# Storing the last image of a dilated convolution: sixteen rows of it cut after partition 119, four rows after partition 123

## The chip, the core and the metric

The kernel runs on one core of a Trainium2 chip. The core has a matrix engine (TensorE, PE in the profile, with its weight loads as PEld), a vector engine (VectorE, DVE), a scalar engine (ScalarE, ACT), a general engine (GpSimd, POOL), a queue engine (SyncE, SP) and 16 DMA engines that move data between the chip's main memory (HBM) and the on-chip memory (SBUF, 128 partitions). Matrix products land in PSUM, also 128 partitions, and are copied from there to SBUF by VectorE or ScalarE.

The metric is the device time of one execution in microseconds, the median of three runs. The profile is one further execution, recorded by the hardware profiler.

## What is computed

A 3 x 3 convolution with dilation 2 and zero padding of 2: 16 images of 64 channels and 64 x 64 pixels, 128 output channels, all in float32 at the ends.

```python
output = np.zeros((batch, c_out, h, w), dtype=np.float32)
for b in range(batch):
    for co in range(c_out):
        for ci in range(c_in):
            for kh in range(k):
                for kw in range(k):
                    output[b, co] += weight[co, ci, kh, kw] * x_pad[b, ci, kh*dilation:kh*dilation+h, kw*dilation:kw*dilation+w]
```

The result is 16 x 128 x 64 x 64 floats, 33.55 MB; the input x is 16.78 MB and the weight 0.29 MB.

## The kernel before

**Tiling.** Images are taken in pairs: the 64 channels of the even image lie on partitions 0 to 63, those of the odd image on 64 to 127, so one pair is a tile of 128 partitions x 4096 floats (`x32`). Eight pairs (`pb` 0 to 7) times four groups of 16 rows (`g` 0 to 3) give 32 rounds `G`. The output tile `o_tiles[pb]` has the 128 output channels on its partitions and both images of the pair one behind the other (`m` 0 and 1), 4096 floats each. So a store of R rows of one image moves, on each partition, R x 64 floats, or R x 256 bytes in one piece.

**A round.** With dilation 2 the rows go in blocks of two, and an output block needs the input blocks before it, at it and behind it. The kernel computes two output blocks (`e` 0 and 1) with five products of the weights in place of six: `psP` is the middle weight row times the sum of an even and an odd block (`rowsum`, line 86, on VectorE); `psA` and `psB` hold the rest for the two (`product`, line 172). ScalarE casts x to float16 (line 74) and copies `psP` to SBUF (line 234); VectorE adds it to `psA` and `psB` and writes the output tile (line 241).

**DMAs.** All of them are issued on SP's queue in the order of the program, which is written by hand (a manual schedule): loads of x (`load`, line 65), stores (`store`, line 186, one per image and range of rows, and `store_both`, line 192, two images in one). `store` takes a list `rows` of partition ranges and issues one DMA for each of them. Each issue waits on SP until what it stores has been written. It also waits until the semaphore that it will count on is free: eight of them are used in turn, so a DMA waits for the one issued eight before it to have landed.

**The last pair.** Pairs 3 to 6 store each image whole when the pair is done (2 MB each). The last pair (`pb` 7, images 14 and 15) stores in halves: at `g` 1 rows 0 to 32 of each image, at `g` 3 rows 32 to 64. Rows 0 to 32 of image 15 go in three DMAs: rows 0 to 24 over all 128 partitions, then rows 24 to 32 (`ROWS4` is 8) over partitions 0 to 123 and over 124 to 127 (`FOUR`, line 197). Rows 32 to 64 of both images then follow over 128 partitions, and nothing comes after them.

Of the kernel before, what the change touches and what calls it, by code (L numbers as in the profile page):

```python
# [10 lines left out]
def kernel(  # L11
# [17 lines left out]
    P = 128  # L29
# [6 lines left out]
    GR = 16  # L36
# [24 lines left out]
    def load(pb, cuts=(0, H)):  # L61
        if pb not in x32_tiles:
            x32_tiles[pb] = fpool.tile([P, HW], f32, tag="x32", name="x32")
        for lo, hi in zip(cuts[:-1], cuts[1:]):
            nc.sync.dma_start(  # L65
                out=x32_tiles[pb][:, lo * W : hi * W], in_=x_pair[pb, :, lo * W : hi * W]
            )
# [10 lines left out]
    def rowsum(c):  # L78
        pb, g = divmod(c, NG)
        if g == 0:  # L80
            xs_tiles[pb] = sxpool.tile([P, HW // 2], f16, tag="xs", name="xs")
        v = x16_tiles[pb][:, g * GR * W : (g + 1) * GR * W].rearrange(
            "p (b e q) -> p b e q", e=2, q=2 * W
        )
        s = xs_tiles[pb][:, g * NH : (g + 1) * NH].rearrange("p (b q) -> p b q", q=2 * W)
        nc.vector.tensor_tensor(out=s, in0=v[:, :, 0], in1=v[:, :, 1], op=add)  # L86
# [67 lines left out]
    def casts(G):  # L154
        for n in range(2 if G else 3):
            c = ahead[0]
            if c >= ngroups or c > G + (7 if c < 2 * NG else 5):
                return
            cast(c)
            ahead[0] += 1  # L160

    def product(ps, src, kind, blk0, nblk, first, last):
        for j in (1, 0, 2):
            dw = (j - 1) * d
            o0, o1 = max(0, -dw), W - max(0, dw)
            t = kind * KW + j
            for hb in range(2):
                pp = slice(hb * CI, (hb + 1) * CI)
                rhs = src(pp, dw + o0, dw + o1)
                po = ps[:, hb * NH + blk0 * 2 * W : hb * NH + (blk0 + nblk) * 2 * W]  # L170
                po = po.rearrange("p (r w) -> p r w", w=W)[:, :, o0:o1]
                nc.tensor.matmul(  # L172
                    out=po,
                    lhsT=w_sb[pp, t * CO : (t + 1) * CO],
                    rhs=rhs,
                    start=first and j == 1,
                    stop=last and j == 2,
                )

    def blocks(x16, b0, n, e):  # L180
        v = x16.rearrange("p (b e r w) -> p b e r w", e=2, r=2, w=W)
        return lambda pp, c0, c1: v[pp, b0 : b0 + n, e, :, c0:c1]

    def store(pb, m, r0=0, r1=H, rows=((0, P),)):
        for lo, hi in rows:
            nc.sync.dma_start(
                out=out_img[2 * pb + m, lo:hi, r0 * W : r1 * W],
                in_=o_tiles[pb][lo:hi, m * HW + r0 * W : m * HW + r1 * W],
            )

    def store_both(pb, r0, r1):
        nc.sync.dma_start(
            out=out_img[2 * pb : 2 * pb + 2, :, r0 * W : r1 * W].rearrange("m o q -> o m q"),
            in_=o_tiles[pb].rearrange("p (m q) -> p m q", m=2)[:, :, r0 * W : r1 * W],
        )

    FOUR = ((0, P - 4), (P - 4, P))
    ROWS4 = 8

    for G in range(ngroups):  # L200
        pb, g = divmod(G, NG)
        x16 = x16_tiles[pb]
        xs = xs_tiles[pb].rearrange("p (r w) -> p r w", w=W)
        if g == 0:
            o_tiles[pb] = opool.tile([P, 2 * HW], f32, tag="osb", name="osb")
        o = o_tiles[pb].rearrange("p (m b e q) -> p m b e q", m=2, e=2, q=2 * W)
        b0 = g * NBLK

        def summed():
            ps = ppool.tile([P, 2 * NH], f32, tag="p", name="psP")  # L210
            sv = lambda pp, c0, c1: xs[pp, g * GR // 2 : (g + 1) * GR // 2, c0:c1]
            product(ps, sv, 0, 0, NBLK, True, True)
            return ps

        if G:
            psP = summed()

        psA = apool.tile([P, 2 * NH], f32, tag="ab", name="psA")
        product(psA, blocks(x16, b0, NBLK, 1), 1, 0, NBLK, True, False)
        z = 1 if g == 0 else 0  # L220
        product(psA, blocks(x16, b0 + z - 1, NBLK - z, 1), 2, z, NBLK - z, False, True)

        psB = apool.tile([P, 2 * NH], f32, tag="ab", name="psB")
        product(psB, blocks(x16, b0, NBLK, 0), 3, 0, NBLK, True, False)
        z = 1 if g == NG - 1 else 0
        product(psB, blocks(x16, b0 + 1, NBLK - z, 0), 4, 0, NBLK - z, False, True)

        if not G:
            psP = summed()

        if not G:
            casts(0)
        p_sb = spool.tile([P, 2 * NH], f32, tag="psb", name="p_sb")
        nc.scalar.copy(out=p_sb, in_=psP)  # L234
        if G:
            casts(G)
        if G + 1 < ngroups:
            rowsum(G + 1)
        pv = p_sb.rearrange("p (m b q) -> p m b q", m=2, q=2 * W)
        for e, ps in ((0, psA), (1, psB)):  # L240
            nc.vector.tensor_tensor(  # L241
                out=o[:, :, b0 : b0 + NBLK, e],
                in0=ps.rearrange("p (m b q) -> p m b q", m=2, q=2 * W),
                in1=pv,
                op=add,
            )

        if G == 0:
            load(XF, (0, H // 2))
        if pb == 0:  # L250
            if g % 2 == 1:
                store_both(0, (g - 1) * GR, (g + 1) * GR)
                if g == 1:
                    load(XF, (H // 2, H))
                else:
                    load(XF + 1)
        elif g == NG - 1 and pb == 1:
            store(1, 0)
            store(1, 1, 0, H // 2)
            load(XF + 2)  # L260
            store(1, 1, H // 2, H)
        elif g == NG - 1 and pb == 2:
            store(2, 0)
            load(XF + 3)
            store(2, 1)
            load(XF + 4)
        elif pb == npairs - 1:
            if g % 2 == 1:
                store(pb, 0, (g - 1) * GR, (g + 1) * GR)
                if g == 1:  # L270
                    store(pb, 1, 0, 2 * GR - ROWS4)
                    store(pb, 1, 2 * GR - ROWS4, 2 * GR, FOUR)
                else:
                    store(pb, 1, (g - 1) * GR, (g + 1) * GR)
        elif g == NG - 1:
            store(pb, 0)
            store(pb, 1)
# [37 lines left out]
```

## Time and profile before

| What | Value |
|---|---|
| median of three runs | 126.85 us (126.62, 126.85, 127.08) |
| the profiled execution's span, first to last instruction | 125.0 us |
| PE busy | 105.8 us (85% of the span) |
| DVE busy | 91.0 us (73%) |
| ACT busy | 64.9 us (52%) |
| HBM read, written | 17.07 MB, 33.55 MB: 405 GB/s over the span |
| DMA packets, mean rate | 4722, 406 GB/s |
| stores of 2 MB, issue to landing | 14.9 us (13 of them) |

The span is measured from the first to the last instruction; the median of the runs is the whole execution as the device counts it, so it is longer. "Issue to landing" is the median time from the DMA's issue on SP to its last piece being counted. A packet is one contiguous piece that one of the 16 DMA engines moves; a DMA also leaves a packet of 4 bytes that counts up its semaphore. The busy share of the 16 engines is written in tenths in each of 40 slices of the span.

### The profile page before, as it was taken

The page shows a single profiled execution, that of the slowest core. Times are in us where ns is not written, and L with a number is a line of the kernel's source. Part 1 is how long each engine was busy: PE and PEld are TensorE (multiplying, and loading weights), DVE is VectorE, ACT ScalarE, POOL GpSimd, SP SyncE. Part 2 cuts the span into 40 slices and gives each one's busy share as a digit, 9 for nine tenths or more (in the row PEclk, how much of TensorE's full clock was granted, in tenths as well). Part 3 has the DMA queues.
Part 4 walks back from the last instruction along what each step waited for, and adds up shares of the span by engine and source line. Part 5 has one row for each costly group of instructions (what it writes and reads, how often), then busy time and mean ns, then how long its engine had stood idle before and what let it go on. Part 6 is the DMA issues. An engine that isn't in the chain of part 4 may idle for free.

```text
span 125.0 us, 2343 instructions
## 1 busy us (share of the span) xinstructions
PE 105.8 (85%) x1002; PEld 57.0 (46%) x1002; DVE 91.0 (73%) x103; ACT 64.9 (52%) x68; POOL 2.2 (2%) x8
## 2 busy tenths in 40 slices
PE   6996999999999999999999999999999999600000
PEld 2353555555555555555555555555555555200000
DVE  0561998988898889888988898889888988700000
ACT  4188896665666566656665666566653333100000
POOL 2400000000000000000000000000000000000000
PEclk9999999999999999999999999999999999985555
DMA  5999999999999999999999999999999999999991
GB/s 142 368 450 435 430 401 315 430 422 420 443 427 435 412 441 438 401 435 435 425 430 427 420 435 430 435 420 435 420 430 430 430 425 435 430 414 412 420 395 73
DMA packets 4722, 50.78 MB, mean 406 GB/s; under 512 B 488, under 2 KB 488, under 8 KB 1000
## 3 DMA queue, kind: packets, MB, share of 16 engines
q1 hardware_dynamic: 4712, 50.63, 96.7%
q8 instruction: 8, 0.13, 0.4%
q14 instruction: 2, 0.02, 0.0%
HBM read 17.07 MB, written 33.55 MB: 405 GB/s over the span
## 4 chain that ended last, share of the span: by engine, by line
PE 76%; DMA 6%; ACT 2%; DVE 1%; DVEq 1%; SPq 1%; issue 0%
PE psA L172 31%; PE psB L172 30%; PE psP L172 16%; DMA x<-in_x_dram 6%; ACT x L74 2%; DVE osb L241 1%; DVEq L310 1%; ACT p_sb L234 1%; SPq L65 0%; SPq L89 0%; DVEq L241 0%
## 5 line engine op out<-in xcount | busy, mean ns | idle before, releaser
L172 PEld LDWEIGHTS <-w_sb 64*128 64x128 f16 x960 | 54.6, 94 | 45.8 <-issue 1.4
L234 ACT COPY p_sb<-psP 128x1024 f32<-128x1024 f32 x32 | 32.4, 1012 | 36.9 <-issue 21.5
L241 DVE TENSOR_TENSOR osb<-psA,p_sb 128x1024 f32<-128x1024 f32 x32 | 39.2, 1225 | 13.4 <-PE psA L172 9.8
L172 PE MATMUL psA<-x,w_sb 64*128 64x496 f16 (+3 forms) x384 | 45.1, 365 | 0.0
L172 PE MATMUL psB<-x,w_sb 64*128 64x496 f16 (+3 forms) x384 | 45.1, 365 | 0.0
L241 DVE TENSOR_TENSOR osb<-psB,p_sb 128x1024 f32<-128x1024 f32 x32 | 39.1, 1222 | 0.0
L74 ACT CAST x<-x 128x1024 f16<-128x1024 f32 (+2 forms) x31 | 32.1, 1044 | 0.5 <-DMA x<-in_x_dram 0.3
L172 PE MATMUL psP<-xs,w_sb 64*128 64x496 f16 (+1 forms) x192 | 26.0, 371 | 1.1 <-ACT p_sb L234 1.1
L86 DVE TENSOR_TENSOR xs<-x 128x512 f16<-128x512 f16 x32 | 13.3, 416 | 0.4 <-ACT x L74 0.4
L102 PE MATMUL dm<-zero 128*128 128x512 f16 x12 | 5.3, 579 | 1.2 <-DVE zero L94 1.2
L102 PEld LDWEIGHTS <-zero 128*128 128x128 f16 x12 | 1.4, 128 | 3.2 <-issue 1.8
L112 DVE CAST wd<-w 128x192 f16<-128x192 f32 x1 | 0.5, 503 | 2.4 <-DMA w<-in_weight_dram 2.4
L125 PEld LDWEIGHTS <-wd 128*64 128x64 f16 x30 | 1.0, 118 | 1.8 <-DVE wd L112 0.8
L137 ACT CAST w_sb<-wt 128x384 f16<-128x384 f32 x1 | 0.5, 478 | 2.3 <-PE wt L125 2.3
L114 ACT ACT_TABLE_LOAD x1 | 1.3, 1283 | 0.7 <-PEq L296 0.7
L125 PE MATMUL wt<-ident,wd 128*64 128x128 f16 x30 | 1.6, 241 | 0.0
L114 ACT CAST wd<-w 128x192 f16<-128x192 f32 x1 | 0.5, 539 | 1.5 <-DMA w<-in_weight_dram 1.5
L139 DVE CAST w_sb<-wt 128x384 f16<-128x384 f32 x1 | 0.6, 557 | 0.7 <-PE wt L125 0.7
L135 DVE CAST w_sb<-wt 128x384 f16<-128x384 f32 x1 | 0.6, 558 | 0.5 <-PE wt L125 0.5
L94 DVE MEMSET zero<- 128x256 uint32 x1 | 0.3, 272 | 0.9 <-PEq L296 0.9
L113 POOL TENSOR_TENSOR wd<-w 128x192 f16<-128x192 f32 x1 | 0.8, 799 | 2.3 <-DMA w<-in_weight_dram 2.3
L116 POOL CAST wd<-w 128x192 f16<-128x192 f32 x1 | 0.8, 806 | 0.0
(11 smaller groups left out, 3.8 us busy)
## 6 DMA issues: line engine op xcount, KB each, us to landing
out_dram<-osb SPq DMA_DIRECT2D x13, 2048.0 KB, 14.9
x<-in_x_dram SPq DMA_DIRECT2D x6, 2048.0 KB, 17.0
out_dram<-osb SPq DMA_DIRECT2D x5, 1024.0 KB, 13.1
x<-in_x_dram SPq DMA_DIRECT2D x2, 1024.0 KB, 13.2
x<-in_x_dram SPq DMA_DIRECT2D x1, 1088.0 KB, 5.6
x<-in_x_dram SPq DMA_DIRECT2D x1, 960.0 KB, 7.4
out_dram<-osb SPq DMA_DIRECT2D x1, 768.0 KB, 15.4
w<-in_weight_dram SPq DMA_DIRECT2D x1, 288.0 KB, 2.8
```

Of the source, the lines that this page charges most:

```text
L74: nc.scalar.copy(out=x16_tiles[pb][:, lo * W : hi * W], in_=x32_tiles[pb][:, lo * W : hi * W])
L86: nc.vector.tensor_tensor(out=s, in0=v[:, :, 0], in1=v[:, :, 1], op=add)
L102: nc.tensor.matmul(out=dm[:, 0:512], lhsT=zero[:, 0:P], rhs=zero)
L113: nc.gpsimd.tensor_tensor(out=wdv[:, 3], in0=wv[:, 0], in1=wv[:, 1], op=sub)
L114: nc.scalar.copy(out=wdv[:, 2], in_=wv[:, 0])
L116: nc.gpsimd.tensor_copy(out=wdv[:, 4], in_=wv[:, 2])
L125: nc.tensor.matmul(out=wts[k % 3][r * CI : (r + 1) * CI, c0 + j * CO : c0 + (j + 1) * CO], lhsT=wd[:, t * CI : (t + 1) * CI], rhs=ident,)
L135: nc.vector.tensor_copy(out=t0[0], in_=t0[1])
L172: nc.tensor.matmul(out=po, lhsT=w_sb[pp, t * CO : (t + 1) * CO], rhs=rhs, start=first and j == 1, stop=last and j == 2,)
L234: nc.scalar.copy(out=p_sb, in_=psP)
L241: nc.vector.tensor_tensor(out=o[:, :, b0 : b0 + NBLK, e], in0=ps.rearrange("p (m b q) -> p m b q", m=2, q=2 * W), in1=pv, op=add,)
L310: with _tile.TileContext(nc) as tc:
```

## The change

Rows 0 to 32 of image 15 go in five DMAs instead of three: rows 0 to 12 over 128 partitions (3 KB on each), rows 12 to 28 over partitions 0 to 119 and over 120 to 127 (4 KB on each), rows 28 to 32 over partitions 0 to 123 and over 124 to 127 (1 KB on each). The same bytes are stored. Nothing else differs on any engine; the lines behind line 197 move down by one, and those behind the stores by three.

```diff
     FOUR = ((0, P - 4), (P - 4, P))
-    ROWS4 = 8
+    FIFTEEN = ((0, P - 8), (P - 8, P))
+    ROWS4, ROWS15 = 4, 16
...
                 store(pb, 0, (g - 1) * GR, (g + 1) * GR)
                 if g == 1:
-                    store(pb, 1, 0, 2 * GR - ROWS4)
-                    store(pb, 1, 2 * GR - ROWS4, 2 * GR, FOUR)
+                    cuts = (0, 2 * GR - ROWS15 - ROWS4, 2 * GR - ROWS4, 2 * GR)
+                    store(pb, 1, cuts[0], cuts[1])
+                    store(pb, 1, cuts[1], cuts[2], FIFTEEN)
+                    store(pb, 1, cuts[2], cuts[3], FOUR)
                 else:
                     store(pb, 1, (g - 1) * GR, (g + 1) * GR)
```

## The prediction

> **What bounds the kernel now.** I read the page's head and its slices first, then its chain, then the end of the timeline, then the waits of SP, then the DMA rows. The page:
>
> ```profile
> span 125.0 us, 2343 instructions
> ...
> DMA  5999999999999999999999999999999999999991
> ...
> DMA packets 4722, 50.78 MB, mean 406 GB/s; under 512 B 488, under 2 KB 488, under 8 KB 1000
> ...
> q1 hardware_dynamic: 4712, 50.63, 96.7%
> ...
> PE 76%; DMA 6%; ACT 2%; DVE 1%; DVEq 1%; SPq 1%; issue 0%
> ...
> out_dram<-osb SPq DMA_DIRECT2D x1, 248.0 KB
> out_dram<-osb SPq DMA_DIRECT2D x1, 8.0 KB
> ```
>
> The chain gives PE 76%, but it starts from the last computing instruction, and that is not the end. The timeline's end, with the SP waits from 95 us on:
>
> ```profile
> 108.25 1.22 DVE L241 TENSOR_TENSOR osb<-psB,p_sb 128x1024 f32<-128x1024 f32 x1
> 109.49 1.08 SPq L186 DMA_DIRECT2D out_dram<-osb  x2
> ...
> SPq L310 <- DMA out_dram<-osb: 13.2, 3, 8.5
> ```
>
> Work on the engines ends at 109.47 us, the last stores are issued by 110.57, and then SP waits 13.2 us for stores to land. The 16 DMA engines are busy from 3 us on and are about 12 to 15 us behind all through the end. So the end is the moment when the *last of the 16* has emptied its queue. Windows one 8 KB packet (0.31 us) wide show them stop one after another:
>
> ```profile
> 120.05:120.36 0.31, 0.00 (x0) 0.00 (x0) 0.00 (x0) 0.00 (x0) 0.00 (x0) 0.50 0.94 396
> ...
> 120.98:121.29 0.31, 0.00 (x0) 0.00 (x0) 0.00 (x0) 0.00 (x0) 0.00 (x0) 0.50 0.82 344
> ...
> 121.91:122.22 0.31, 0.00 (x0) 0.00 (x0) 0.00 (x0) 0.00 (x0) 0.00 (x0) 0.50 0.44 185
> ...
> 122.84:123.15 0.31, 0.00 (x0) 0.00 (x0) 0.00 (x0) 0.00 (x0) 0.00 (x0) 0.50 0.25 106
> ...
> 123.46:123.77 0.31, 0.00 (x0) 0.00 (x0) 0.00 (x0) 0.00 (x0) 0.00 (x0) 0.50 0.07 26
> ```
>
> The last two columns are the share of 16 engines and GB/s. GB/s x 0.31 us / 8192 B is the packets begun, so the engines still at work: 15, 13, 7, 4, 1. Three us pass between the first engine out and the last.
>
> **Which engine is late.** The 124-row and the 4-row store use four engines each: every store leaves one packet of 4 B for each engine that it uses, and 488 such packets are 30 DMAs x 16 + 2 x 4. 124 and 4 rows are 31 and 1 on each of four. In the trace's packet records each packet starts 3 to 4 ns before the one ahead of it on its engine ends, so the records can be followed engine by engine. Four chains carry the 31 + 1 packets of 2 KB, the same four for both stores; I call them the four. Ends of the chains' last packets, us:
> - the four: 122.92, 123.50, 123.69, 123.82
> - one slow engine: 123.46
> - eleven others: 120.36, 120.62, 120.92, 121.74, 121.83, 121.90, 122.10, 122.12, 122.16, 122.53, 122.62
>
> The trace has the landings 0.33 us behind these (0.47 for the slow engine): the four land last at 124.14, the slow one at 123.93, the others by 122.97, and the span ends at 124.97, so 0.83 us behind the last landing. The slow engine's 16 KB packets took 634 to 662 ns, instead of 611, in stores (not loads) up to 108.7 us, while the computing engines worked; after that 611 again. Its lag is made before the changed stores run (from about 113 us); it only carries through.
>
> **Prices.** Packet times in the records: 2 KB 84 ns, 6 KB 234, 8 KB 309, 16 KB 611, the 4 B packet 9. They lie on a line, 8.7 ns + 37.6 ns per KB. The change brings three sizes that the trace lacks. 4 KB: between half of 8 KB (155) and twice 2 KB (168), I take 159. 3 KB: between 117 and 126, I take 122. 1 KB: between half of 2 KB (42) and a whole 2 KB packet (84), I take 46, since even the 4 B packet costs only 9.
>
> **The change, part by part**, for rows 0 to 32 of image 15, in ns on each engine:
> - Removed: 8 packets of 6 KB + 9 = 1881 on all 16; 32 of 2 KB + 18 = 2706 on the four. So the four 4587, the others 1881.
> - Added: 8 packets of 3 KB + 9 = 985 on all. 120 rows of 4 KB over 15 engines, 8 each: 1272 + 9 = 1281. 8 rows of 4 KB on eight engines: 159 + 9 = 168. 124 and 4 rows of 1 KB: 32 x 46 + 18 = 1490 on the four.
> - With the four first, numbered 0 to 3: the four 985 + 1281 + 168 + 1490 = 3924, **-663**. Engines 4 to 7: 2434, **+553**. 8 to 14: 2266, **+385**. Engine 15: 985, **-896**.
>
> That 120 rows go over 15 and 8 rows over 8 is a choice: 124 -> 4, 4 -> 4, 128 -> 16 fit "the largest divisor up to 16", and also "the largest power of two that divides" (rival b). I take the first: 31 rows on one engine show that shares need not be round numbers, so I expect no such rule for the count of engines either. The Trainium skill, "DMA: Bandwidth & Descriptors", section "Why a DMA increments its semaphore by 16 and not by 1", has the first: the largest k up to 16 that divides the slowest dimension of both sides, its example 100 partitions on 10, and the lowest-numbered k. The 488 agrees with it, 15 engines no run here shows; by the other reading the sum would be the rival's.
>
> New ends. The four: 124.14 - 0.66 = 123.48. The eleven: at most 122.97 + 0.39 to 0.55 = 123.36 to 123.52. The slow engine, if it is number 15: 123.93 - 0.90 = 123.03. The last landing moves from 124.14 to about 123.5: **-0.63 us**.
>
> **What else it adds.** Two more issues on SP's queue, 0.64 to 0.73 us each by the four rows around them (starts 103.6, 104.29, 105.07): the group ends at about 107.3 instead of 105.8. SP's next issue waits for the last addition at 109.47, so 2.2 us of cover remain; without it each would delay the last stores by 0.7.
> Each DMA also waits until the semaphore it takes, one of eight in turn, is free of the DMA eight before. The last two stores took two whose users landed at 99.6 and 104.8, long before 109.49. Two places further they take those of image 12 and 13's stores (issued 97.12 and 97.50), landing 109.86 and 114.73. The first costs 0.4 us of issue. The second moves the *last store's issue* from 109.9 to 114.7. Nothing is queued behind it on SP but the closing wait. Its packets can reach the engines 1.0 us after issue starts (the first DMA: 0.74 to 1.757), so by about 116. The engines begin the last store's packets only from 117.9 (the first out at 120.36 less 8 x 309 ns) and, if a fast engine were spared 0.9 us, from 117.0. Cost nothing, with 1 us of cover; to set the end it would have to land some 5 us later.
> The small transfers themselves: the 8 KB one landed on the four 0.19 us behind the 124-row one in the trace, of which 84 + 9 are its packet and its 4 B. So up to 0.1 us a transfer is unexplained: twice that, on engines 0 to 7, is +0.2 at most. I take 0. The Trainium skill, same page, section "Rules for kernel authors", speaks against such transfers: under 64 KB one pays mostly overhead, and its fixed cost of about 2 us each, estimated for two more in a row, would make about 130.9 us. The 0.19 us contradicts it for transfers behind a full queue.
>
> **Sum.** 125.0 - 0.63 = 124.3 of span; with the 1.9 us that the median (126.85) has beyond the profiled span, **126.2 us**.
>
> **Rivals.**
> (a) The slow engine is one of 4 to 14. Then it gets +0.39 or +0.55 and lands at 124.31 or 124.48: +0.17 or +0.34, **127.0 to 127.2**. For: it is not of the four, and twelve numbers are left. Against: the lag may be the profiled execution's own; and if the engines' first packets (1.757 to 2.143 us) go out in order of number, as three of the four among the first seven suggest, its first one is thirteenth or later. Chains through the first 20 us are not sure, so this is weak. The Trainium skill, same page, section "Latency and other measured facts", has engines 7 and 15 as usually slower: 15 would give my sum, 7 the 127.2. The trace shows one slow engine, not two.
> (b) Slower: 120 rows go over eight engines. 15 packets of 4 KB on engines 0 to 7: 2385 + 9 instead of 1281. The four: +450, landing at 124.59; 4 to 7: +1666, from 122.97 up to 124.64, or 125.6 with the slow one there. +0.5 to 1.5: **127.3 to 128.3**. For: 124 -> 4. It decides as soon as fewer than 15 engines share the 120 rows.
> (c) Slower: 1 KB packets cost as much as 2 KB ones. 32 x 38 = +1216 on the four: 124.70, **127.4**. Against: the line through four sizes and the 9 ns.
> (d) Little moves: without the profiler another engine is last (one that an instruction fetch of 0.95 us hit late, as at 107.98), and the four had slack. Such an engine, of 8 to 14 and landing at 123.4 to 123.75 instead of the 122.97, would go to 123.79 to 124.14, where the four are now. The gain falls to 0.35 or nothing: **126.5 to 126.85**.
>
> **Chances.** Forecast 0.62, (a) 0.17, (b) 0.07, (c) 0.04, (d) 0.10. A measurement here can tell about 0.3%, 0.38 us (the three runs lie within 0.46). Forecast is faster by more, except 0.02 of it; (a) is mostly within; (b) and (c) are slower, and 0.03 of (a). So 0.60 faster, 0.26 same, 0.14 slower. The likeliest's own range is 125.9 to 126.5: 0.9 is the most that any engine is relieved. The range goes up to 127.1, which takes in (d) and most of (a).
>
> **What would show it.** Packets under 512 B: 30 x 16 + 15 + 8 + 4 + 4 = 511 with 15 engines, 504 with (b). Engines still at work 0.6 us before the last landing: more than the four or five of now, since three groups end near 123.5. If one alone stays to 124.3 or later, it is (a); four there, (c). If the last store's wait counts, all 16 engines have a gap at 116 to 118 us. The prediction is wrong if the last landing does not come before 123.8 us in a span like this one.

## The result and the profile after

The changed kernel is slower. Eight runs of it have a median of 128.37 us (127.68 to 128.74) against 127.03 us for eight runs of before; the ratio is 1.0105, with a 95% interval of 1.0077 to 1.0134. The prediction was 126.2 us. Some executions run a few per cent longer than the rest (before: up to 130.25 us); medians here are over all runs, ratios over the others alone. The profiled execution's span went from 125.0 to 126.4 us.

The lines of the page that answer to those shown of before (the last three are from the view of DMA issues; its columns are the same):

```profile
span 126.4 us, 2345 instructions
...
DMA  4999999999999999999999999999999999999970
...
DMA packets 4873, 50.78 MB, mean 402 GB/s; under 512 B 511, under 2 KB 639, under 8 KB 1151
...
q1 hardware_dynamic: 4863, 50.63, 95.9%
...
PE 75%; DMA 6%; ACT 2%; DVE 1%; DVEq 1%; SPq 1%; issue 0%
...
out_dram<-osb SPq DMA_DIRECT2D x1, 124.0 KB
out_dram<-osb SPq DMA_DIRECT2D x1, 32.0 KB
out_dram<-osb SPq DMA_DIRECT2D x1, 4.0 KB
```

The same bytes are moved. Packets under 512 B are 511, which is 30 x 16 + 15 + 8 + 4 + 4: the 120 rows did go over 15 engines and the 8 rows over 8. The end of the timeline, and the waits of SP from 105 us on (us in total, times, longest):

```profile
108.68 1.22 DVE L242 TENSOR_TENSOR osb<-psB,p_sb 128x1024 f32<-128x1024 f32 x1
110.48 5.15 SPq L186 DMA_DIRECT2D out_dram<-osb  x2
...
SPq L313 <- DMA out_dram<-osb: 9.8, 2, 6.8
SPq L186 <- DMA out_dram<-osb: 7.6, 2, 4.4
```

Computing ends at 109.90, and the issuing of the two last stores now takes 5.15 us from the start of the first to the end of the second: the last one waited 4.4 us for an earlier store to land, as forecast, and went out at 115.3. The end is again the wait for the last landing (6.8 us). How the engines stop, in windows one 8 KB packet wide (the last two columns are the share of the 16 engines and GB/s):

```profile
120.05:120.36 0.31, 0.00 (x0) 0.00 (x0) 0.00 (x0) 0.00 (x0) 0.00 (x0) 0.50 1.00 423
...
121.91:122.22 0.31, 0.00 (x0) 0.00 (x0) 0.00 (x0) 0.00 (x0) 0.00 (x0) 0.50 0.63 264
122.84:123.15 0.31, 0.00 (x0) 0.00 (x0) 0.00 (x0) 0.00 (x0) 0.00 (x0) 0.50 0.44 185
...
124.08:124.39 0.31, 0.00 (x0) 0.00 (x0) 0.00 (x0) 0.00 (x0) 0.00 (x0) 0.50 0.13 53
124.39:124.70 0.31, 0.00 (x0) 0.00 (x0) 0.00 (x0) 0.00 (x0) 0.00 (x0) 0.50 0.06 26
```

That is 16, 10, 7, 2 and 1 engines: at 122.84 to 123.15 seven instead of four, and the last one 1.3 us later than before. Where it came from shows in 2 us windows. Before:

```profile
114.00:116.00 2.00, 0.00 (x0) 0.00 (x0) 0.00 (x0) 0.00 (x0) 0.00 (x0) 0.50 1.00 418
116.00:118.00 2.00, 0.00 (x0) 0.00 (x0) 0.00 (x0) 0.00 (x0) 0.00 (x0) 0.50 1.03 426
118.00:120.00 2.00, 0.00 (x0) 0.00 (x0) 0.00 (x0) 0.00 (x0) 0.00 (x0) 0.50 1.04 435
```

After:

```profile
114.00:116.00 2.00, 0.00 (x0) 0.00 (x0) 0.00 (x0) 0.00 (x0) 0.00 (x0) 0.50 0.98 404
116.00:118.00 2.00, 0.00 (x0) 0.00 (x0) 0.00 (x0) 0.00 (x0) 0.00 (x0) 0.50 1.04 385
118.00:120.00 2.00, 0.00 (x0) 0.00 (x0) 0.00 (x0) 0.00 (x0) 0.00 (x0) 0.50 1.02 386
```

All engines are as busy as before (shares of 1.02 to 1.04), but from 116 to 120 us they move 385 GB/s in place of 430. So the packets themselves last longer. In the packet records 27 packets between 116.2 and 119.8 us are stretched, by 5.9 us in all: 20 of the 128 of 4 KB took 185 to 1192 ns, where the other 108 took 159, with four of 3 KB and three of 8 KB. Before had no stretched packet after 109 us. The 1 KB packets took 46 ns and the 3 KB ones 121, as worked out. As far as the chains can be followed through that stretch, the engine that ends last is one of those without a share of the 8 rows, and its eight 4 KB packets took 3.55 us instead of 1.24. The stretched packets fall mostly on engines that come late to the store: of the five that come first none has one, and before the first stretched packet of any engine 58 packets of 4 KB ran at their usual time.

### The profile page after: what moved, and what is told of

Its sections match the earlier page's. It is cut to its first block, busy times and chain, and to the rows that moved or that the text cites. A ratio compares the mean times of both kernels' runs of the same rounds, so it can differ in the third digit from the quotient of the medians.

```text
span 126.4 us, 2345 instructions
## 1 busy us (share of the span) xinstructions
PE 106.3 (84%) x1002; PEld 56.9 (45%) x1002; DVE 91.1 (72%) x103; ACT 65.1 (52%) x68; POOL 2.2 (2%) x8
## 4 chain that ended last, share of the span: by engine, by line
PE 75%; DMA 6%; ACT 2%; DVE 1%; DVEq 1%; SPq 1%; issue 0%
PE psA L172 30%; PE psB L172 29%; PE psP L172 16%; DMA x<-in_x_dram 6%; ACT x L74 1%; DVE osb L242 1%; DVEq L313 1%; ACT p_sb L235 1%; SPq L65 0%; SPq L89 0%; DVEq L242 0%
```

## The experiments

A packet is called stretched here if it took more than 12 ns over the line of prices; the slow engine's 634 to 662 ns are not counted, nor the packets beside an instruction fetch. Times are medians. Ratios are against before on the same chip, with their 95% intervals; where no ratio stands, it is a single run.

**The parts one by one.** The whole rows without any split, which says what before's own split is worth:

```diff
-                    store(pb, 1, 0, 2 * GR - ROWS4)
-                    store(pb, 1, 2 * GR - ROWS4, 2 * GR, FOUR)
+                    store(pb, 1, 0, 2 * GR)
```

> Rows 0 to 32 of image 15 in one store over 128 partitions, no split at all. It measures what the split of before is worth. If the slow engine is not one of the four, it moves 8 packets of 8 KB (8 x 306 + 6 = 2453 ns) where it moved 8 of 6 KB (1857): its landing goes from 123.93 to 124.53, 0.39 us behind before: 127.2 to 127.4 if the slow engine is late without the profiler too. If its lag belongs to the profiled execution alone, the latest of the other twelve, 122.97 + 0.60 = 123.57, sets the end: about 126.4.

Measured: 127.59 us, 1.0031 (1.0002 to 1.0060), no stretched packet. The slow engine ended alone, 0.75 us behind the next. So it is late without the split, and relieving it is worth some 0.4 us by the ratio and 0.7 by the medians (before had 126.89); that fits the first of the two cases.

The 120 and 8 alone:

```diff
-                    store(pb, 1, 0, 2 * GR - ROWS4)
-                    store(pb, 1, 2 * GR - ROWS4, 2 * GR, FOUR)
+                    store(pb, 1, 0, 16)
+                    store(pb, 1, 16, 32, ((0, P - 8), (P - 8, P)))
```

> Rows 0 to 16 over 128 partitions, rows 16 to 32 over 0 to 119 and over 120 to 127; nothing over 124 and 4. Three DMAs as before, so the last stores are issued as early as before, and no packet of 1 KB. Theory P (120 rows on 15 engines are dealt out of step with 128 rows on 16; engines meet on the same rows and 4 KB packets stretch): slower than before by 0.8 to 1.5 us, stretched packets of 4 KB as in the changed kernel, GB/s at 116 to 120 us under 400. Theory S (the 1 KB packets disturb the others) and theory L (the last store, issued 5 us late, disturbs them): no stretched packets, and by counting the latest engine of 8 to 14 gets 2498 ns where it had 1857: +0.4 us if the slow one is among them, faster by 0.3 or more if it is number 15.

Measured: 127.60 us, 1.0053 (1.0023 to 1.0082); four stretched packets, all of the 4 KB that the partition cut brings (232 to 519 ns), 1.0 us in all. Stretching appears without the 1 KB packets and without the late issue, so theory P has its first support, but weaker than it said: the rate at 116 to 120 us did not fall (426 and 418 GB/s). Nor does the time speak for it: the slow engine ends last here, with none of its own packets stretched, and by counting its 17 packets of 4 KB take 0.8 us more than the eight of 6 KB in before. The slow engine was told here by its landings, some 0.15 us later after its last packet than the others', and it was the last of the eight that shared the 8-row store: its number is under 8. This sign is not a safe one (in the changed kernel's trace the slow engine's landings come no later than the others'), so the number is counted further below.

The four rows alone:

```diff
-    ROWS4 = 8
+    ROWS4 = 4
```

> Before with 4 rows instead of 8 over 124 and 4 partitions (1 KB packets), and nothing over 120 and 8. Three DMAs as before. Theory S: stretched packets beside the 1 KB ones, slower than before by 0.5 us or more. Theories P and L: no stretched packets; the four are relieved of 0.9 us, all others get 0.3 us more: last landing 124.2 against 124.14 in the profile, time within 0.4 us of before.

Measured: 126.93 us, 1.0013 (0.9983 to 1.0042), no stretched packet. Theory S alone is out.

The late issue alone:

```diff
-                    store(pb, 1, 0, 2 * GR - ROWS4)
+                    store(pb, 1, 0, 8)
+                    store(pb, 1, 8, 16)
+                    store(pb, 1, 16, 2 * GR - ROWS4)
                     store(pb, 1, 2 * GR - ROWS4, 2 * GR, FOUR)
```

> Before, with its rows 0 to 24 of image 15 cut into three stores over 128 partitions (8, 8 and 8 rows) in place of one. Two DMAs more, as in the changed kernel, so the last two stores wait for the same earlier stores and the very last is issued near 115 us; the dealing over engines is that of before, and all other sizes too. Theory L: stretched packets from about 116 us on and 0.8 to 1.5 us slower. Theories P and S: no stretched packets, within 0.3 us of before.

Measured: 127.11 us, 1.0001 (0.9974 to 1.0027); the last store was issued at 114.98, and one packet was 14 ns long. Theory L is out, and two DMAs more along the rows cost nothing that can be told.

**Which engine is slow.**

```diff
-            store(pb, 1)
+            if pb == 5:
+                store(pb, 1, rows=((0, 5), (5, 12), (12, 21), (21, 32), (32, P)))
+            else:
+                store(pb, 1)
```

> Before, with image 11 (the second of pair 5) stored in five DMAs of 5, 7, 9, 11 and 96 partitions instead of one of 128. It tells the slow engine's number. If a DMA of k rows uses the engines 0 to k-1, and 96 rows go 6 to each of 16, the packets of 16 KB that an engine moves for that image are 10 on engines 0 to 4, 9 on 5 and 6, 8 on 7 and 8, 7 on 9 and 10, 6 on 11 to 15. The slow engine's packets are told by their 634 to 662 ns. My forecast had 6 (number 15). The second run, where the slow engine's landing comes last among the eight engines of the 8-row store, says 8 to 10 (number 4 to 7). Counts that do not fit 10, 9, 8, 7 and 6 packets would say that the dealing is not so.

Measured: 131.34 us (before 126.92). The slow chain, as start:size:ns, from the end of the store ahead through the five ("s" is the 4 B packet that closes a store):

```
98857:16K:653 99506:s 99512:16K:642 100151:s 100157:16K:652 100805:s 100811:16K:652 101459:s
101465:16K:633 102095:s 102100:16K:638 102735:16K:634 103365:16K:672 104033:16K:644 104664:16K:644 105295:16K:653 105944:s
```

It has one packet of each of the stores of 5, 7, 9 and 11 rows and six of the 96: ten, so it is among the first five. It carries none of before's 124-row packets, so it is not among the first four: **number 4**. The 16 chains together fit ten, nine, eight, seven and six packets on 5, 2, 2, 2 and 5 engines. The slow engine kept its 644 ns through the 96 rows, which start at partition 32, so the slowness seems to go with the engine and not with certain rows. The run brought more than it was made for: 38 packets of 16 KB over 700 ns at 90 to 114 us (2 in before).

**The parts together.** The change without its 124 and 4, but as late:

```diff
-                    store(pb, 1, 0, 2 * GR - ROWS4)
-                    store(pb, 1, 2 * GR - ROWS4, 2 * GR, FOUR)
+                    store(pb, 1, 0, 12)
+                    store(pb, 1, 12, 28, ((0, P - 8), (P - 8, P)))
+                    store(pb, 1, 28, 30)
+                    store(pb, 1, 30, 32)
```

> The changed kernel without its 124 and 4: rows 28 to 30 and 30 to 32 each go over 128 partitions, so it has as many DMAs and its last store is issued as late (near 115 us); rows 0 to 12 and the 120 and 8 are those of the change. If the late issue makes the 4 KB packets of the 120-row store stretch more (27 stretched in the changed kernel, 4 in the second run): 15 or more, GB/s at 116 to 120 us under 400, and 128 us or more. If the 1 KB packets do: about 4 stretched packets as in the second run, and 127.3 to 127.8 us.

Measured: 128.31 us, 1.0101 (1.0038 to 1.0164), eight stretched packets, 1.3 us. It fits neither case: the packets say that the late issue is not it, and the time is as long as the change's. What I had not counted is that without the 124 and 4 nothing relieves the slow engine: 8 x 118 + 8 x 155 + 161 + 16 x 24 and some closing packets are about 2.75 us where before has 1.86, so 0.9 us more. That is not the whole of it either: in this run's trace, as far as the chains can be followed, number 4 empties its queue at 124.13, and the engine that ends last, at 125.14, is one of those without a share of the 8 rows, with five of the eight stretched packets. So a few stretched packets are enough where they fall on a late engine.

The change with its last two stores in one, so that none is late:

```diff
                 else:
-                    store(pb, 1, (g - 1) * GR, (g + 1) * GR)
+                    store_both(pb, (g - 1) * GR, (g + 1) * GR)
```

(and the store of image 14 only at `g` 1)

> The changed kernel with its last two stores (rows 32 to 64 of image 14, of image 15) as one DMA of both images, so that it waits for the store that landed at about 110 us and no DMA is issued late; the packets on each engine are the same. If the late issue makes the difference: under 10 stretched packets, 127.3 to 127.8 us. If the 1 KB packets beside the 120-row store do: 20 or more stretched packets, 128 us or more.

Measured: 128.46 us, 1.0107 (1.0071 to 1.0144), 34 stretched packets, 5.4 us. As slow as the change: the late issue has no part in it, and the 120-row store with the 124-row store behind it stretches 27 and 34 packets, where the 120-row store without it stretched 4 and 8.

All engines equally loaded, but dealt otherwise:

```diff
-                    store(pb, 1, 0, 2 * GR - ROWS4)
-                    store(pb, 1, 2 * GR - ROWS4, 2 * GR, FOUR)
+                    store(pb, 1, 0, 16)
+                    store(pb, 1, 16, 32, ((0, P - 16), (P - 16, P)))
```

> Rows 0 to 16 over 128 partitions, rows 16 to 32 over 0 to 111 and over 112 to 127. Both use all 16 engines, 7 rows and 1 row on each, so every engine moves the same number of 4 KB packets as without any split: no engine is relieved or burdened, but engines work on other partitions than in a store of 128. Theory P (dealing out of step makes engines meet): stretched 4 KB packets, and slower than the run without a split (127.59 us). If what hurts is only that 15 engines share 120 rows (a number that does not divide 128, one engine left out): no stretched packets and 127.4 to 127.8 us, as without a split.

Measured: 127.78 us, 1.0049 (1.0013 to 1.0085), eight stretched packets of 4 KB (200 to 598 ns), 1.5 us. The packets speak for theory P; the time can't be told from the run without a split (1.0031).

The change with 8 rows over 124 and 4, which spares the slow engine:

```diff
-    ROWS4, ROWS15 = 4, 16
+    ROWS4, ROWS15 = 8, 16
```

> The changed kernel with 8 rows instead of 4 over 124 and 4 (2 KB packets, as before), so rows 0 to 8 go over 128, 8 to 24 over 120 and 8, 24 to 32 over 124 and 4. The slow engine, number 4 by the count of the fifth run, then gets 8 packets of 2 KB, 8 + 1 of 4 KB: 641 + 6 + 1248 + 161 = 2056 ns, 0.2 us over before's 1857, instead of 0.5; the four get 2056 + 2572 = 4628, 0.2 us over before's 4423. If the change is slow because the slow engine is burdened: 127.0 to 127.3 us. If the stretched packets (120-row store beside the 124-row one) make the end: 20 or more stretched, and 127.8 us or more.

Measured: **129.85 us, 1.0209 (1.0155 to 1.0263)**, about 80 stretched packets, 16 us. Its windows:

```profile
116.00:118.00 2.00, 0.00 (x0) 0.00 (x0) 0.00 (x0) 0.00 (x0) 0.00 (x0) 0.50 0.98 307
118.00:120.00 2.00, 0.00 (x0) 0.00 (x0) 0.00 (x0) 0.00 (x0) 0.00 (x0) 0.50 1.00 356
```

307 and 356 GB/s with every engine busy. The slow engine has less to move than in the change, the four only 0.2 us more than in before, and the time is twice as far off. This is the run that decides between the burden and the stretching: less burden and more stretching made it slower, so here the stretching makes the end.

**The dealing by itself, in a larger store.** Image 11, amid stores of 128 partitions, cut over the partitions only (2 MB, 16 KB packets):

```diff
-            store(pb, 1)
+            store(pb, 1, rows=((0, P - 8), (P - 8, P)) if pb == 5 else ((0, P),))
```

> Before, with image 11 (the second of pair 5) stored whole in two DMAs, partitions 0 to 119 and 120 to 127, instead of one. The dealing of the change with packets of 16 KB, amid stores of 128. If dealing a store differently makes engines meet: stretched 16 KB packets between 97 and 108 us (96 rows and four small ones gave 29, 12.8 us in sum). It is the reference for the next two.

Measured: 134.37 us (before 127.01), 69 packets over 700 ns at 90 to 114 us. The 12 us around it, before and here (before the GB/s stands the busy share):

```profile
96.00:108.00 12.00, 12.00 (x118) 6.49 (x114) 10.26 (x11) 4.05 (x4) 0.00 (x0) 1.00 1.00 426
```

```profile
96.00:108.00 12.00, 12.00 (x120) 6.48 (x116) 10.26 (x12) 4.05 (x4) 0.00 (x0) 1.00 1.00 332
```

Next, where the engines meet. The same two DMAs, with their places shifted by 8 on one side only:

```diff
-            store(pb, 1)
+            if pb == 5:
+                for (a, b), (lo, hi) in zip(((0, 120), (120, 128)), ((8, 128), (0, 8))):
+                    nc.sync.dma_start(out=out_img[2 * pb + 1, lo:hi], in_=o_tiles[pb][a:b, HW:])
+            else:
+                store(pb, 1)
```

(the second run has the two lists of ranges in `zip` exchanged)

> As the run before, but partitions 0 to 119 go to output channels 8 to 127 of image 11 and partitions 120 to 127 to channels 0 to 7: its output rows of that image are shifted by 8 channels. Each engine reads the same partitions as in the run before and writes 8 channels further. If engines meet in SBUF: as many stretched packets as in the run before. If they meet in HBM, on the rows of the output: clearly other (half or double).

> The opposite: partitions 8 to 127 go to channels 0 to 119 and partitions 0 to 7 to channels 120 to 127 of image 11. Each engine writes the same channels as two runs before and reads 8 partitions further; the output of that image is shifted by 8 channels. If engines meet in SBUF: clearly another number of stretched packets than there (half or double). If in HBM: as many.

Measured: 133.50 and 136.01 us, 64 and 67 packets over 700 ns. Neither half nor double of 69 in either, so the two runs do not tell SBUF from HBM.

Dealing without imbalance, 112 and 16, then 64 and 64:

```diff
-            store(pb, 1)
+            store(pb, 1, rows=((0, P - 16), (P - 16, P)) if pb == 5 else ((0, P),))
```

(and with `P // 2` in the place of `P - 16`)

> Before, with image 11 stored in two DMAs of 112 and 16 partitions: 7 and 1 packets of 16 KB on each of 16 engines, so no engine gets ahead or behind (120 and 8 left number 15 with none and 0 to 7 with nine). If the stretched packets come from rows being dealt to other engines than in a store of 128: 30 or more packets over 700 ns at 90 to 114 us (69 with 120 and 8, 2 before), and some us longer. If they come from engines being thrown out of balance: a few at most, and within 0.5 us of before.

> Before, with image 11 stored in two DMAs of 64 partitions: 4 and 4 packets of 16 KB on each of 16 engines. Balanced too. If any cut over partitions deals rows to other engines and stretches packets: 30 or more over 700 ns. If halves of 64 keep to the same engines' rows: as before, 2.

Measured: 130.93 and 131.57 us (before 126.85), 43 and 66 packets over 700 ns. The same 12 us, first 112 and 16, then 64 and 64:

```profile
96.00:108.00 12.00, 12.00 (x120) 6.46 (x115) 10.26 (x12) 4.05 (x4) 0.00 (x0) 1.00 1.01 360
```

```profile
96.00:108.00 12.00, 12.00 (x118) 6.35 (x114) 10.27 (x11) 4.05 (x4) 0.00 (x0) 1.00 1.01 340
```

Every engine has exactly its eight packets, and 360 and 340 GB/s are left of 426. So it is not the imbalance that 15 engines leave; what these runs share is the cut over the partitions. Each is a single run, but all six with image 11 cut have 38 or more packets over 700 ns, where before has 2. That such a cut hurts because it deals the rows to the engines otherwise than the stores beside it is the likeliest reading, but no record names the partitions of a packet, so it is argued and not shown. Engines that get in each other's way within the cut store alone are not ruled out. The nearest control, image 11 cut in two along its rows, was not run; the last pair's store cut that way stretched next to nothing.

**A version that might beat both**, 6 rows instead of 8 in before:

```diff
-    ROWS4 = 8
+    ROWS4 = 6
```

> Before with 6 rows instead of 8 over 124 and 4 (1.5 KB packets), as a version that may beat both: by the profiles of 8 and 4 rows the four end 0.5 us earlier than with 8 and the slow engine 0.15 us later. No stretched packets; 126.5 to 126.9 us, that is the same as before to 0.3% faster.

Measured: 126.94 us, 1.0013 (0.9984 to 1.0042), no stretched packet. No gain; nothing tried beats the kernel before.

## Why the prediction failed

- **What bounds the kernel**: right. In both kernels the end is the last DMA engine to empty its queue, and SP's closing wait shows it.
- **How many engines** share 120, 8, 124 and 4 rows: right, 15, 8, 4 and 4 (511 small packets). Rival (b) is out.
- **Packet prices** of 46, 122 and 159 ns: right for an undisturbed packet (46, 121 and 159). Rival (c) is out.
- **The late last issue**: right. It moved from 109.9 to 115.3 and cost nothing (1.0001 with it alone; 1.0107 for the change without it).
- **"The slow engine, if it is number 15"**: wrong. It is number 4. The change gave it 553 ns more instead of 896 less; by counting that is rival (a) at its upper price, 127.2 us. The order of first packets, which I took as weak support for a high number, misled. The Trainium skill ("DMA: Bandwidth & Descriptors", section "Latency and other measured facts") names engines 7 and 15 as the usual slow ones, with a best guess at the reason that holds for DMAs issued from GpSimd alone. Here all are issued on SP, and the slow one is neither of the two.
- **"120 rows of 4 KB over 15 engines, 8 each: 1272 + 9"**: this is the second term that failed, and no rival had it. The term took the price of a packet as a property of its size. In the trace 20 of the 128 packets of 4 KB took up to 7.5 times that, and the runs show when: a store cut over the partitions, between stores that are not, stretches packets while all engines stay busy (image 11 cut at 120, 112 and 64), and in the last pair most of all when two such cuts run together (4 and 8 stretched packets with the 120 and 8 alone, 27 to some 80 with the 124 and 4 behind it).

How the 1.34 us divide can only be bounded. With the slow engine burdened by 0.60 us and nothing stretched (no split at all) the time rose by 0.31%, 0.4 us (0.7 by the medians); the change burdens it by 0.55. So some 0.4 to 0.7 us may be the burden and the rest, 0.6 to 1 us, the stretching; with the burden cut to 0.2 us but more stretching, the loss grew to 2.7 us. In the changed kernel's own trace the engine that ends last is a stretched one and not number 4, which ended 1.2 us earlier.

That trace also holds something like rival (d). An engine with no stretched packet at all, one of 8 to 14, empties its queue at 124.37, 0.75 us before the last one and 0.56 behind the last of before. It moves the 0.39 us more that the prediction counted for its group, and it had come late: its first 8 KB packet of the last pair starts at 114.82, that of the latest engine in before, the slow one, at 114.24. Why it came late was not traced. So in this one execution the stretching moved the end by 0.75 us at most.

Before's own 124-row store shows no stretched packet in its profile nor in the profiles with 4 and 6 rows, though it too is dealt otherwise. In the runs with image 11 cut, the same store did have stretched packets, so it seems to depend on how the engines stand to each other when it comes. Nor is stretching peculiar to cut stores: at 48 to 52 us, where loads and stores over all 128 partitions are under way together, before has four packets of 16 KB over 700 ns and the changed kernel 13. What they meet on, and why four engines alone do no harm, stays open: the two shifted runs did not tell, and nothing finer was tried.

## What to carry to other kernels

To even out DMA engines by cutting a store over partitions, count more than bytes per engine: the cut can stretch the packets themselves. With 2 MB cut into 64 and 64 partitions the rate fell from 426 to 340 GB/s with every engine busy. The Trainium skill (same page, section "Rules for kernel authors") advises one 128-partition transfer in place of two halves because halves gain nothing; here, in a single run, they lost. A share of 1.0 with falling GB/s is the sign to look for. And find the late engine's number first: stores of 5, 7, 9, 11 and 96 rows narrow it to two or five in one profile.

## What the runs showed beside

- One DMA engine of 16 is 5% slower (634 to 662 ns for 16 KB instead of 611), only in stores and only while the engines compute, in the profiled runs. It is number 4 by the count of one run; the changed kernel's trace agrees as far as it goes, for there the slow engine moves nine packets of 4 KB and none of 1 KB, as numbers 4 to 7 do. Without its relief the unprofiled time is 0.31% longer, which suggests that it is late there too.
- More DMAs behind a full queue are cheap if they are cut along the rows: three of 256 KB instead of one of 768 cost nothing that can be told (1.0001, 0.9974 to 1.0027).
